# Making the two parts of w_out beside the projections, and sharing out the turned weights' parts anew

## The chip, the cores and the metric

One core of one Trainium2 chip runs the whole step as one program. The metric is the device time in microseconds (us) of one execution; what is compared are medians of several executions.

The engines are TensorE (PE, its weight loads PEld), VectorE (DVE), ScalarE (ACT), GpSimd (POOL) and SyncE (SP), which issues all DMAs of this kernel. Each engine works through its own instructions in one fixed order; an instruction whose input isn't there holds up all that stand behind it on that engine.

## The reference, cut to what matters

One layer of a hybrid backbone on 256 context tokens and 1024 latent tokens, width 1024. A combined projection of the normed input feeds a gated linear attention (GLA) and a differential attention; both are gated, concatenated and pass through one output projection:

```python
def diff_attention(q, k, v, lam):
    ...
        s = jnp.einsum('bqhid,bkhid->bihqk', qi, k).astype(jnp.float32) * scale
        p = jax.nn.softmax(s, axis=-1)
        a = p[:, 0] - lam * p[:, 1]
        return jnp.einsum('bhqk,bkhv->bqhv', a.astype(v.dtype), v)
...
    o = jnp.concatenate([og, od], axis=-1) * jax.nn.silu(gate)
    return jnp.einsum('blm,md->bld', o, w_out_l)
```

Everything is fp32. The kernel gets near fp32 precision from matmuls in a reduced fp32 format (F32R) by splitting each operand x into two parts, hi = F32R(x) and lo = F32R(x - hi), and adding three products: hi·hi, hi·lo and lo·hi.

## The kernel before, in words

**Stages.** A start (modulation, norm, the turned and split input `hhi`, `hlo`), then three mixes of projection work with GLA and other work (`MIX[0]` to `MIX[2]`, lines 1284 to 1300), then the attention of the latent tokens, into whose end the output projection reaches, and the rest of the output tiles.

**A mix.** `mix` takes one step of the generator named by each letter of a string: m is the projections (a unit of w_in is loaded, split and multiplied), a the GLA and the context tokens' attention, b a third one. In `MIX[1]` b is `cached()` (line 662): eight times it loads 256 KB of cached keys or values into `kqst` (tag s1), splits them with `split_store` (line 593: ACT copies to hi, the engine passed to it subtracts to lo, two DMAs store the parts to memory), in buffers of tags h1 and h2. These three tags have two buffers each, and the projections' own results pass through them. In the mixes a scheduler puts each engine's instructions in order, the strings giving the priority; `MIX[2]` has no b.

**The attention** (lines 1303 to 1508) is ordered by hand: with `manual_schedule` each engine keeps the order in which the instructions are written. Sixteen blocks (4 heads, 4 times 256 query tokens) are pipelined: iteration j goes through the tuple `ORDER`, and each step is done for block j plus its offset. A block has the scores (`score`, L1130), the maxima (`peak`, L1137, DVE), the exponentials (`expo`, L1142, ACT), the difference of the two maps (`combine`: L1149, L1150 and the long L1152, all DVE), and then six pairs of key tiles, 0 to 5. For each pair `turn` transposes on PE into one PSUM tile `tp` and `part` makes hi (`aTh`) and lo (`aTl`); `weigh` then multiplies them with the values. The tuple `PARTS` says who does it. With 'direct' ACT reads `tp` into hi and DVE subtracts from `tp`. Otherwise ACT first copies `tp` to `aT` (L1167, three buffers), the first letter says who makes hi from it (G: POOL, L1178; A: ACT, L1176) and the second who makes lo (L1181; G: POOL, V: DVE). `late` takes the second six entries for the last five blocks. The merge of a block has two POOL steps, `oc` (L1219, `merge4`) and `olo` (L1225, `merge5`).

In `ORDER` the steps that use POOL or feed it stand like this, with pair 2 turned at an iteration's very end and parted at the next one's very beginning:

```python
    ('part', -2, 2), ('weigh', -2, 0), ('slot', 0), ('turn', -2, 3), ('part', -2, 1), ...
    ('merge4', -3), ... ('part', -2, 4), ... ('merge5', -3), ... ('part', -2, 5), ... ('wo', 0, 8, 6, 14),
    ('turn', -1, 0), ... ('weigh', -2, 10), ('part', -1, 0), ('weigh', -2, 11), ...
    ('score', 0, 1, 1), ... ('merge1', -2), ('expo', 0, 1, 0), ('turn', -1, 2),
```

(`('part', -2, 3)` stands just before `('merge4', -3)`.) The two `wo` steps call `load_wo` in iterations 6 to 13: a DMA of 256 KB of w_out into a buffer of the ring of `aT`, then `woh` and `wol` on POOL (L1310, L1311), sixteen times in all. `FILL` says where matmuls of the output tiles are put between the steps, from iteration 16 on.

Of the kernel before, what the change touches and what calls it, by code (L numbers as in the profile page):

```python
# [101 lines left out]
def mix(pattern, main, *others):  # L102
# [4 lines left out]
    for g in gens.values():  # L107
# [14 lines left out]
    ('mmmmabmmmmammammbmammmmammmmabmbbmmmmmambambmmmmammmbmmmbmmbmamamammbmmbbmmabmmamammmmmbmm'),  # L122
    ('mmamamaaammaaabmmmmaaammaaambmmaammabmabaammaambamammbmmabammmmabammmamamaaaammabaabmaamma'),
    ('ammmmmmammammamaamammammmmaammammmammmamammammmmmammmmaammmmmmammmmammmamamamammmaammammmammmmmmamam'
     'aammmmmamammmammmammammmmmammmmaammmamammmaamammammmmmammammammmmaamammmmaaammmaaaammaaammmmamaamaaa'
     'mmamaaamaammaaamaaammamamamaaamaaamammmaaaamaamaaaaaamaammmmaaamammaammmamm'),
)

PARTS = ('direct', 'GG', 'AV', 'GG', 'GG', 'GG', 'direct', 'GG', 'AV', 'GG', 'GG', 'AG')

ORDER = (
    ('part', -2, 2), ('weigh', -2, 0), ('slot', 0), ('turn', -2, 3), ('part', -2, 1), ('slot', 0), ('merge2', -3),
# [45 lines left out]
def body(tc, nc, I, O, ctx):  # L178
# [33 lines left out]
    qs_d = [dram.tile([2, 2, P, NTOK], F32, name=f"qs_d{i}") for i in range(2)]  # L212
    vs_d = dram.tile([2, NKALL, 512], F32, name="vs_d")
    oh_d = dram.tile([2, 8, P, NTOK], F32, name="oh_d")


    def sigmoid_parts(dst, x, tmp):
# [17 lines left out]
    with psum:  # L235
# [429 lines left out]
        def cached():  # L665
# [6 lines left out]
            for t in range(4):  # L672
# [3 lines left out]
                split_store(r, [rows[0], rows[1]], 0, 512, 1.0, G)  # L676
                yield

        def modgate():

            ga = gp.tile([P, 2, 2, 512], F32, name="ga", tag="W", bufs=2)
            acc = [[ga[:, j, hf] for hf in range(2)] for j in range(2)]
            for kt in range(KT):
                wg = gp.tile([P, 2, 512], F32, name="wg", tag="att", bufs=2)
                for hf in range(2):
                    S.dma_start(wg[:, hf], I["w_mod"][kt * P:(kt + 1) * P, 2 * D + hf * 512:2 * D + (hf + 1) * 512])
                for j in range(2):
                    for hf in range(2):
                        src = wg[:, hf]
                        if kt == 0:  # L690
                            V.tensor_scalar(out=acc[j][hf], in0=src, scalar1=sic[:, kt, j:j + 1], scalar2=None,
                                            op0=ALU.mult)
                        else:
                            V.scalar_tensor_tensor(out=acc[j][hf], in0=src, scalar=sic[:, kt, j:j + 1],
                                                   in1=acc[j][hf], op0=ALU.mult, op1=ALU.add)
                yield
            for j in range(2):
                for hf in range(2):
                    cs = slice(hf * 512, (hf + 1) * 512)
                    ps = psL.tile([P, 2, 512], F32, name="gs", tag="lv")[0:1, 0]  # L700
                    T.matmul(ps, one, acc[j][hf], start=True, stop=True)
                    row = sp.tile([1, 512], F32, name="grow", tag="s2")
                    S.dma_start(row, I["bgate"][:, cs])
                    V.tensor_tensor(out=row, in0=ps, in1=row, op=ALU.add)
                    S.dma_start(ga_d[j:j + 1, cs], row)
                    yield
# [403 lines left out]
        class Block:  # L1110


            def __init__(self, job):
                self.h, self.c0, self.nk = job[:3]
                self.job = job
                self.npair = self.nk // 256
                self.late = 6 * (jobs.index(job) >= 11)

            def load(self):
                self.ks, self.vs = get_kv(self.job)  # L1120
# [34 lines left out]
            def turn(self, pr):  # L1155

                tp = psT.tile([P, 512], F32, name="tp")
                for i in range(2):
                    kt = pr * 2 + i
                    for qt in range(2):  # L1160
                        T.transpose(tp[:, i * N + qt * P:i * N + (qt + 1) * P], self.am[qt][:, kt * P:(kt + 1) * P], ident)  # L1161
                if PARTS[pr + self.late] == "direct":
                    full, hi = tp, ap_.tile([P, 512], F32R, name="aTh", bufs=5)
                    A.activation(hi, tp, AF.Copy)
                else:
                    full, hi = ap_.tile([P, 512], F32, name="aT", bufs=3), None
                    A.activation(full, tp, AF.Copy)  # L1167
                self.full[pr] = full, hi

            def part(self, pr):  # L1170

                full, hi = self.full.pop(pr)
                if hi is None:
                    hi = ap_.tile([P, 512], F32R, name="aTh", bufs=5)
                    if PARTS[pr + self.late][0] == "A":
                        A.activation(hi, full, AF.Copy)  # L1176
                    else:
                        G.tensor_scalar(out=hi, in0=full, scalar1=1.0, scalar2=0.0, op0=ALU.mult, op1=ALU.add)  # L1178
                lo = ap_.tile([P, 512], F32R, name="aTl", bufs=5)
                eng = G if PARTS[pr + self.late][1] == "G" else V  # L1180
                eng.tensor_tensor(out=lo, in0=full, in1=hi.bitcast(F32), op=ALU.subtract)  # L1181
                self.ab[pr] = hi, lo

# [78 lines left out]
        def first_block():  # L1262

            b = blocks[0]
            for qt in range(2):
# [21 lines left out]
                *[feat_unit(U_G + m, use_gate(m)) for m in range(4, 6)],  # L1287

                last_gates()),
            seq(backward, stagger([prompt(0), prompt(1)], PL), stagger([prompt(2), prompt(3)], PL), first_loads(), first_block(), prompt_gate()))  # L1290
        proj.close()
    psum.close()
    with ExitStack() as s3:
# [8 lines left out]
        def load_wo(m, hf):  # L1302
# [2 lines left out]
                wol[m] = wo.tile([P, D], F32R, name=f"wol{m}")  # L1305
            cs = slice(hf * 512, (hf + 1) * 512)
            hi, lo = woh[m][:, cs], wol[m][:, cs]
            r = ap_.tile([P, 512], F32, name="wo_r", tag="aT", bufs=3)
            S.dma_start(r, I["w_out"][SLOT[m] * P:(SLOT[m] + 1) * P, cs])
            G.tensor_scalar(out=hi, in0=r, scalar1=1.0, scalar2=0.0, op0=ALU.mult, op1=ALU.add)  # L1310
            G.tensor_tensor(out=lo, in0=r, in1=hi.bitcast(F32), op=ALU.subtract)  # L1311


        s3b = ExitStack()
# [221 lines left out]
```

## Time and profile before

| what | value |
|---|---|
| median of 3 runs | 982.35 us (981.92 to 984.94) |
| the profiled execution's own time | 980.46 us |
| its span, first to last instruction | 978.4 us |
| PE busy | 907.6 us, 93% of the span |
| DVE busy | 607.8 us, 62% |
| ACT busy | 461.1 us, 47% |
| POOL busy | 410.6 us, 42% |
| DMA | 157.91 MB, 160 GB/s over the span |

The shares are means over stages that have different limits: POOL is 42% busy in the whole, but 88% and more in slices 24 to 33 of the 40 into which the page cuts the span. The time is read stage by stage, and in the attention cycle by cycle.

### The profile page before, as it was taken

What the parts mean: (1) busy time and instruction counts of PE and PEld (TensorE: products, weight loads), DVE (VectorE), ACT (ScalarE), POOL (GpSimd) and SP (SyncE); (2) the same over time, 40 slices, a digit from 0 to 9 for tenths busy, and PEclk for the clock granted to TensorE, in tenths of its full rate; (3) what the DMA queues carried; (4) which work ended last, traced back from release to release, by engine and by line L of the source; (5) the groups of instructions that cost most, each with busy time, mean ns of one, the idle gap of its engine ahead of it and who ended that gap; (6) DMA issues with size and microseconds to landing.
All of it is one profiled execution on the core that took longest, in us unless ns stands there. A gap on an engine that the chain in (4) does not pass through costs nothing.

```text
span 978.4 us, 15886 instructions
## 1 busy us (share of the span) xinstructions
PE 907.6 (93%) x5894; PEld 766.4 (78%) x5894; DVE 607.8 (62%) x853; ACT 461.1 (47%) x882; POOL 410.6 (42%) x344
## 2 busy tenths in 40 slices
PE   6889999998999999899899999899988888999997
PEld 1489889976899897677787888788867677888886
DVE  3788952232267655876675646899888889722223
ACT  2454355344522323233334666687767677732122
POOL 0454223135302213342334000488999999752221
PEclk9899999999999999999999999999999999999999
DMA  8842754587744454453464563363345226137751
GB/s 292 324 151 73 225 172 131 151 266 240 253 151 124 149 160 140 132 165 115 135 202 150 191 213 99 113 185 104 118 163 142 84 80 210 43 108 235 232 167 65
DMA packets 146316, 157.91 MB, mean 161 GB/s; under 512 B 10168, under 2 KB 115768, under 8 KB 146240
## 3 DMA queue, kind: packets, MB, share of 16 engines
q1 hardware_dynamic: 146240, 156.91, 50.8%
q8 instruction: 46, 0.75, 0.3%
q14 instruction: 30, 0.25, 0.1%
HBM read 104.30 MB, written 52.57 MB: 160 GB/s over the span
## 4 chain that ended last, share of the span: by engine, by line
PE 51%; POOL 13%; DVE 11%; issue 10%; ACT 7%; DMA 6%; SPq 1%; POOLq 0%; ACTq 0%; DVEq 0%
PE acc L452 4%; PE acc L453 4%; PE acc L454 4%; PE sc L1347 4%; PE sc L1348 4%; PE sc L1349 4%; PE acc L528 3%; PE acc L530 3%; PE acc L529 3%; POOL aTh L1178 3%; PE lv L831 3%; ACT p L1142 3%; PE mp L324 3%; POOL wol L1311 2%; POOL woh L1310 2%
## 5 line engine op out<-in xcount | busy, mean ns | idle before, releaser
L452 PE MATMUL acc<-hhi,w_hi 128*128 128x512 f32 (+1 forms) x440 | 158.2, 359 | 0.0
L453 PE MATMUL acc<-hlo,w_hi 128*128 128x512 f32 (+1 forms) x440 | 156.2, 355 | 0.0
L454 PE MATMUL acc<-hhi,w_lo 128*128 128x512 f32 (+1 forms) x440 | 155.8, 354 | 0.0
L1137 DVE TENSOR_REDUCE sm<-sc 128x1 f32<-128x1536 f32 x60 | 105.0, 1752 | 12.1 <-PE sc L1130 12.1
L1130 PE MATMUL sc<-ks,q 128*128 128x512 f32 x360 | 98.0, 408 | 2.7 <-ACT p L1142 2.7
L1142 ACT ACTIVATE p<-sc,sm 128x1536 f32<-128x1536 f32 x60 | 92.4, 1539 | 9.1 <-DVE sm L1137 6.4
L528 PE MATMUL acc<-w_hi,hhi 128*128 128x256 f32 x320 | 93.6, 293 | 2.5 <-ACT kqst L477 2.4
L1181 POOL TENSOR_TENSOR aTl<-aT,aTh 128x512 fp32r<-128x512 f32 x64 | 93.7, 1464 | 4.9
L452 PEld LDWEIGHTS acc<-hhi,w_hi 128*128 128x128 f32 x440 | 83.6, 190 | 12.8 <-issue 1.9
L454 PEld LDWEIGHTS acc<-hhi,w_lo 128*128 128x128 f32 x440 | 83.4, 190 | 11.4 <-issue 0.2
L530 PE MATMUL acc<-w_hi,hlo 128*128 128x256 f32 x320 | 92.0, 288 | 0.0
L529 PE MATMUL acc<-w_lo,hhi 128*128 128x256 f32 x320 | 91.9, 287 | 0.0
L453 PEld LDWEIGHTS acc<-hlo,w_hi 128*128 128x128 f32 x440 | 83.7, 190 | 10.4 <-issue 0.2
L1178 POOL TENSOR_SCALAR aTh<-aT 128x512 fp32r<-128x512 f32 x59 | 61.2, 1037 | 39.5 <-ACT aT L1167 38.0
L1130 PEld LDWEIGHTS sc<-ks,q 128*128 128x128 f32 x360 | 64.2, 191 | 13.7 <-ACT p L1142 3.0
L528 PEld LDWEIGHTS acc<-w_hi,hhi 128*128 128x128 f32 x320 | 62.7, 196 | 8.1 <-ACT kqst L477 2.6
L1167 ACT ACTIVATE aT<-tp 128x512 f32<-128x512 f32 x80 | 47.8, 598 | 39.9 <-PE tp L1161 19.0
L1161 PE MATMUL tp<-ident,p 128*128 128x128 f32 x360 | 54.7, 274 | 11.8 <-ACT aT L1167 11.8
L1347 PE MATMUL sc<-woh,oh 128*128 128x512 f32 (+1 forms) x168 | 65.0, 387 | 0.0
L1349 PE MATMUL sc<-woh,oh 128*128 128x512 f32 (+1 forms) x168 | 64.6, 384 | 0.0
L1348 PE MATMUL sc<-wol,oh 128*128 128x512 f32 (+1 forms) x168 | 64.6, 384 | 0.0
L1192 PE MATMUL ov<-aTl,vs 128*128 128x256 f32 x192 | 56.3, 293 | 8.3 <-POOL aTl L1181 7.7
(309 smaller groups left out, 2128.1 us busy)
## 6 DMA issues: line engine op xcount, KB each, us to landing
w_raw<-w_u SPq DMA_DIRECT2D x29, 512.0 KB, 3.6
oh<-oh_d SPq DMA_DIRECT2D x20, 512.0 KB, 4.2
wm<-w_mod SPq DMA_DIRECT2D x16, 512.0 KB, 5.0
q<-qs_d SPq DMA_DIRECT2D x64, 128.0 KB, 2.9
ks<-ks_d SPq DMA_DIRECT2D x4, 1536.0 KB
vs<-vs_d SPq DMA_DIRECT2D x8, 768.0 KB, 5.6
xt<-x_all SPq DMA_DIRECT2D x10, 512.0 KB, 10.2
x<-x_all SPq DMA_DIRECT2D x10, 512.0 KB, 4.7
```

The source lines that it names most:

```text
L452: T.matmul(ps, w_h, hhi[bi][:, kt, ts], start=kt == 0, stop=False)
L453: T.matmul(ps, w_h, hlo[bi][:, kt, ts], start=False, stop=False)
L454: T.matmul(ps, w_l, hhi[bi][:, kt, ts], start=False, stop=kt == KT - 1)
L528: T.matmul(ps, h_h, w_h, start=kt == 0, stop=False)
L529: T.matmul(ps, h_h, w_l, start=False, stop=False)
L530: T.matmul(ps, h_l, w_h, start=False, stop=kt == KT - 1)
L1130: T.matmul(sc[:, k0:k0 + w], self.q[:, a, sub, qt * P:(qt + 1) * P], self.ks[:, sub, k0:k0 + w], start=a == 0, stop=a == 1)
L1137: V.tensor_reduce(out=self.sm[qt][:, sub:sub + 1], in_=self.sc[qt, sub], op=ALU.max, axis=AX.X, negate=True)
L1142: A.activation(p_, self.sc.pop((qt, sub)), AF.Exp, bias=sm[:, sub:sub + 1], accum_out=self.s0[:, qt:qt + 1] if sub == 0 else sm[:, 2:3])
L1347: T.matmul(ps, oh[:, 0, m], woh[m][:, cs], start=m == 0, stop=False)
L1348: T.matmul(ps, oh[:, 0, m], wol[m][:, cs], start=False, stop=False)
L1349: T.matmul(ps, oh[:, 1, m], woh[m][:, cs], start=False, stop=m == 7)
```

## The change

A generator `wo_parts` is added as b of `MIX[2]`, where sixteen b's are set into the unchanged row of m's and a's. It loads each half row block of w_out, splits it with `split_store` (hi on ACT, lo on POOL) and stores both parts to memory (`wo_d`). `load_wo` brings the two parts back with two DMAs of 256 KB and does no arithmetic. `PARTS` has one set of six entries for all blocks: pair 2 goes from 'AV' to 'GG', and pair 5 from 'GG' to 'AG' (which the last five blocks had already).

```diff
-PARTS = ('direct', 'GG', 'AV', 'GG', 'GG', 'GG', 'direct', 'GG', 'AV', 'GG', 'GG', 'AG')
+PARTS = ('direct', 'GG', 'GG', 'GG', 'GG', 'AG')
...
+    wo_d = dram.tile([2, 8, P, D], F32, name="wo_d")
...
+        def wo_parts():
+
+            for m in range(8):
+                for hf in range(2):
+                    r = sp.tile([P, 512], F32, name="kqst", tag="s1")
+                    cs = slice(hf * 512, (hf + 1) * 512)
+                    S.dma_start(r, I["w_out"][SLOT[m] * P:(SLOT[m] + 1) * P, cs])
+                    split_store(r, [wo_d[0, m], wo_d[1, m]], hf * 512, 512, 1.0, G)
+                    yield
...
-                self.late = 6 * (jobs.index(job) >= 11)
...
-                if PARTS[pr + self.late] == "direct":
+                if PARTS[pr] == "direct":
...
-                    if PARTS[pr + self.late][0] == "A":
+                    if PARTS[pr][0] == "A":
...
-                eng = G if PARTS[pr + self.late][1] == "G" else V
+                eng = G if PARTS[pr][1] == "G" else V
...
-            r = ap_.tile([P, 512], F32, name="wo_r", tag="aT", bufs=3)
-            S.dma_start(r, I["w_out"][SLOT[m] * P:(SLOT[m] + 1) * P, cs])
-            G.tensor_scalar(out=hi, in0=r, scalar1=1.0, scalar2=0.0, op0=ALU.mult, op1=ALU.add)
-            G.tensor_tensor(out=lo, in0=r, in1=hi.bitcast(F32), op=ALU.subtract)
+            S.dma_start(hi.bitcast(F32), wo_d[0, m, :, cs])
+            S.dma_start(lo.bitcast(F32), wo_d[1, m, :, cs])
```

In `MIX[2]` the first b stands after 70 m's and 31 a's, the last after 151 of 164 m's and 100 of 111 a's. `ORDER` and `FILL` are as before.

## Rows read from the trace of the kernel before

**Rows 1.** The page, part 2: busy tenths of POOL in 40 slices
```profile
POOL 0454223135302213342334000488999999752221
```

**Rows 2.** Windows cut at starts of the aTh behind oc; busy us by engine
```profile
core 0: us, PE busy (x) PEld busy (x) DVE busy (x) ACT busy (x) POOL busy (x), PEclk, DMA share, GB/s
629.67:643.64 13.97, 13.55 (x92) 12.21 (x91) 13.62 (x16) 11.76 (x20) 11.56 (x9) 1.00 0.93 264
643.64:687.69 44.05, 41.45 (x272) 36.80 (x271) 39.51 (x43) 35.68 (x61) 35.51 (x30) 1.00 0.42 129
687.69:822.91 135.22, 117.14 (x728) 98.86 (x727) 116.51 (x113) 97.10 (x162) 128.41 (x112) 1.00 0.41 124
822.91:836.91 14.00, 13.16 (x86) 11.61 (x85) 13.09 (x15) 11.70 (x22) 11.30 (x10) 1.00 0.54 168
836.91:866.52 29.61, 29.61 (x194) 26.59 (x193) 16.57 (x20) 19.48 (x36) 22.28 (x19) 1.00 0.09 28
```

**Rows 3.** Timeline of POOL: its first step in the attention, and one cycle
```profile
start us, us, engine line op out<-in xcount [idle before <-releaser]
622.83 0.62 POOL L1178 TENSOR_SCALAR aTh<-aT 128x512 fp32r<-128x512 f32 x1 [26.32 <-ACT aT L1167]
...
675.11 1.29 POOL L1181 TENSOR_TENSOR aTl<-aT,aTh 128x512 fp32r<-128x512 f32 x1
676.37 0.74 POOL L1225 TENSOR_TENSOR olo<-oc,ohi 128x256 fp32r<-128x256 f32 x1
677.07 0.62 POOL L1178 TENSOR_SCALAR aTh<-aT 128x512 fp32r<-128x512 f32 x1
677.78 1.27 POOL L1181 TENSOR_TENSOR aTl<-aT,aTh 128x512 fp32r<-128x512 f32 x1
679.10 0.62 POOL L1178 TENSOR_SCALAR aTh<-aT 128x512 fp32r<-128x512 f32 x1
679.80 2.69 POOL L1181 TENSOR_TENSOR aTl<-aT,aTh 128x512 fp32r<-128x512 f32 x1
683.90 0.62 POOL L1178 TENSOR_SCALAR aTh<-aT 128x512 fp32r<-128x512 f32 x1 [1.41 <-ACT aT L1167]
684.60 1.28 POOL L1181 TENSOR_TENSOR aTl<-aT,aTh 128x512 fp32r<-128x512 f32 x1
686.90 0.74 POOL L1219 TENSOR_TENSOR oc<-oc,gt 128x256 f32<-128x256 f32 x1 [1.01 <-DVE sm L1149]
```

**Rows 4.** Timeline of ACT, the same stretches
```profile
624.67 0.60 ACT L1167 ACTIVATE aT<-tp 128x512 f32<-128x512 f32 x1
...
679.90 0.38 ACT L1200 ACTIVATE oc<-ov 128x256 f32<-128x256 f32 x1 [0.88 <-PE ov L1192]
680.18 1.54 ACT L1142 ACTIVATE p<-sc,sm 128x1536 f32<-128x1536 f32 x1
...
681.81 0.60 ACT L1167 ACTIVATE aT<-tp 128x512 f32<-128x512 f32 x1
```

**Rows 5.** Timeline of DVE, the same cycle
```profile
679.54 1.82 DVE L1152 SCALAR_TENSOR_TENSOR p<-p,sm,p 128x1536 f32<-128x1536 f32 x1
...
683.17 0.69 DVE L1181 TENSOR_TENSOR aTl<-aT,aTh 128x512 fp32r<-128x512 f32 x1
...
686.39 0.43 DVE L1218 TENSOR_TENSOR oc<-oc,sq 128x256 f32<-128x256 f32 x1
```

**Rows 6.** Timeline of PE, the same cycle
```profile
679.10 0.39 PE L1192 MATMUL ov<-aTl,vs 128*128 128x256 f32 x1 [0.48 <-POOL aTl L1181]
...
687.71 0.29 PE L1192 MATMUL ov<-aTl,vs 128*128 128x256 f32 x1
```

**Rows 7.** Groups of instructions by line: busy us, mean ns, idle us before them
```profile
L1311 POOL TENSOR_TENSOR wol<-wo_r,woh 128x512 fp32r<-128x512 f32 x16 | 23.6, 1476 | 1.3
L1310 POOL TENSOR_SCALAR woh<-wo_r 128x512 fp32r<-128x512 f32 x16 | 19.3, 1204 | 0.0
...
L600 POOL TENSOR_TENSOR klo<-kqst,khi 128x512 fp32r<-128x512 f32 x8 | 11.3, 1415 | 19.3 <-ACT khi L598 19.3
...
L598 ACT ACTIVATE khi<-kqst 128x512 fp32r<-128x512 f32 x8 | 5.0, 629 | 7.3 <-DMA kqst<-cv 4.4 <-DMA kqst<-ck 2.9
```

**Rows 8.** Windows, columns as in Rows 2: the cached parts' stretch, and the changed mix
```profile
200.00:262.00 62.00, 57.30 (x331) 44.82 (x330) 19.46 (x39) 30.67 (x56) 23.10 (x19) 1.00 0.79 260
430.00:590.00 160.00, 152.70 (x990) 129.00 (x989) 102.97 (x158) 70.82 (x148) 38.07 (x28) 0.99 0.52 165
```

More of the change, by code (lines that the diff above doesn't have):

```diff
@@ L124 @@
     ('ammmmmmammammamaamammammmmaammammmammmamammammmmmammmmaammmmmmammmmammmamamamammmaammammmammmmmmamam'
-     'aammmmmamammmammmammammmmmammmmaammmamammmaamammammmmmammammammmmaamammmmaaammmaaaammaaammmmamaamaaa'
-     'mmamaaamaammaaamaaammamamamaaamaaamammmaaaamaamaaaaaamaammmmaaamammaammmamm'),
+     'abammmmmamambmmammmammabmmmmmammmmbaammmamammbmaamammammbmmmammammabmmmmaamammbmmaaammmaabaammaaammm'
+     'bmamaamaaambmamaaamaambmaaamaaammbamamamaaambaaamammmaabaamaamaaaabaamaammmmaaamammaammmamm'),
 )
-PARTS = ('direct', 'GG', 'AV', 'GG', 'GG', 'GG', 'direct', 'GG', 'AV', 'GG', 'GG', 'AG')
+PARTS = ('direct', 'GG', 'GG', 'GG', 'GG', 'AG')
 ORDER = (
@@ L1289, in body @@
                 last_gates()),
-            seq(backward, stagger([prompt(0), prompt(1)], PL), stagger([prompt(2), prompt(3)], PL), first_loads(), first_block(), prompt_gate()))
+            seq(backward, stagger([prompt(0), prompt(1)], PL), stagger([prompt(2), prompt(3)], PL), first_loads(), first_block(), prompt_gate()), wo_parts())
         proj.close()
```

## The prediction, made before the changed kernel ran

> **What bounds the kernel now.** I read the page's row of busy tenths first: POOL stands at 8 and 9 only in slices 24 to 33, the attention; elsewhere it has room [rows 1]. There I cut windows at the start of the first aTh behind oc, once in each iteration, so that a window's length is a cycle's length [rows 2]. The first cycle (iteration 2 to 3) lasts 13.97 us, the next three 44.05 / 3 = 14.68, the eight that make parts of w_out 135.22 / 8 = 16.90, the one behind them 14.00; the last two (29.61 us) hold matmuls of the output tiles, and PE is busy all through. That is 207.2 us for 13 cycles. In the eight POOL is busy 128.41 of 135.22 us and PE 117.14: POOL is the bound. In the others PE is nearest to it (41.45 of 44.05) with DVE close (39.51), and POOL has 2.8 us of idle time a cycle. What the loads of w_out cost today is thus 8 × (16.90 - 14.68) = 17.8 us, and that is the most that taking them away could give by itself.
>
> In one such cycle I then read who waits for whom. In order of time POOL does [rows 3]: lo of pair 4 (675.11), olo, pair 5 (677.07 and 677.78), then at once pair 1 (679.10, 679.80), a wait of 1.41 us for ACT, pair 3 (683.90, 684.60), oc. Pair 2 isn't there: it is ACT's and DVE's (DVE 683.17, [rows 5]). Two things matter. First, lo of pair 1 took 2.69 us and not 1.28. DVE's L1152 had started at 679.54 while hi of pair 1 ran (to 679.72), ended at 681.36, and POOL's waiting lo was through at 682.49: the two don't run together, and the one that waits goes ahead of the other's next step. It costs POOL 2.69 - 1.28 = 1.41 us. Second, pair 2's copy aT, the last step of an iteration's turns, ran 681.81 to 682.41 [rows 4], 3.36 us behind the end of pair 5's lo (677.78 + 1.27 = 679.05). That is no accident: PE waits for that lo (679.10, 0.48 us idle [rows 6]), does the rest of pair 5, ACT then copies the block's sum (oc, 679.90), does an exponential (680.18), and only then comes that aT.
>
> **The attention, part by part.** Removed: woh and wol, 16 × (1.20 + 1.48) = 42.9 us of POOL [rows 7]. Added: hi and lo of pair 2 on POOL, 16 × (0.62 + 1.28) = 30.4 us; removed for pair 5: 11 × 0.62 = 6.8 us. By sums of busy time POOL loses 19 us, and DVE 16 × 0.69 = 11 us. But `ORDER` is unchanged, and in it pair 2's part is the first step of an iteration, ahead of pair 1's. Today this costs POOL nothing. Now POOL does hi of pair 2 first, and that needs the aT that comes 3.36 us behind lo of pair 5. Pair 1, which today fills this gap, is queued behind it, and pairs 3 and 4, oc, olo and pair 5's lo behind that. So each cycle holds a closed loop: aT of pair 2, all eleven POOL steps, lo of pair 5, PE, ACT, the next aT of pair 2. Its length from the rows:
>
> - from aT's end to POOL's start 0.09 us (as at 683.90, with pair 3's aT);
> - 4 hi at 0.70 from start to start (677.07 to 677.78), 5 lo at 1.26 (675.11 to 676.37), olo 0.70, oc 0.75: 2.80 + 6.30 + 1.45 = 10.55 us [rows 3];
> - one L1152 in this stretch, 1.41 us. It can't fall into the gap, as it waits for L1218, which stands 3.98 us behind aT's end (686.39 - 682.41), when POOL is at work. The other L1152 of the iteration falls into the gap (today 679.54, 0.49 behind lo of pair 5). L1218 itself (0.43 us) holds POOL some 0.3 us [rows 5];
> - back from lo of pair 5 to aT: 3.36 us.
>
> Sum 15.7 us. It hangs on one tie. Pair 3's hi is due at 0.09 + 2 × (0.70 + 1.26) = 4.01, L1218 at 3.98. If L1218 comes first, L1152 gets in ahead of pair 3's lo, which is then done some 7.7 us behind aT; PE wants it 5.3 us behind (687.71 - 682.41 [rows 6]) and, with its other waits, about 6.3 to 6.9. That stall of about 0.8 us is passed on to the cycle: 16.5. I take 15.9, between the two and nearer to the sum. Bounds: 14.00, the shortest that a cycle has been with pair 5's hi on ACT, and 16.90, a cycle with both parts of w_out. So 13 cycles take 13 × 15.9 = 206.7 us against 207.2: the eight long cycles give back what the five short ones lose. -0.5 us, with ends 13 × 14.0 - 207.2 = -25 and 13 × 16.9 - 207.2 = +12.5.
>
> At the attention's start POOL's first hi waits for pair 2's aT, 624.67 + 0.60 + 0.09 = 625.36, and not for pair 1's at 622.83 [rows 3, 4]: +2.5 us (0 to 3). In the last two cycles PE is full today [rows 2]; the loop, with fewer exponentials in it, is about as long as they are, and I take +1.5 (0 to 3). The attention in all: +3.5 us.
>
> The Trainium skill weighs on this (SBUF — State Buffer, Who interferes with whom): a DVE instruction with two SBUF inputs and a GpSimd one that reads SBUF exclude each other for the whole instruction. The 2.69 us agrees. The lo of pair 2 on DVE was such an instruction, so by the rule moving it to POOL spares POOL up to 0.69 us a cycle, 9 us over 13. By the row it spares nothing in a short cycle: at 683.17 POOL was waiting for ACT until 683.90.
>
> **The loads back.** 32 DMAs of 256 KB in place of 16, in iterations 6 to 13, straight into their own tiles: 8 MB in 135 us, where the DMA engines are 41% busy [rows 2]. The output tiles need them long after, so 0. That a load no longer takes a buffer of the ring of aT is part of the 17.8 us.
>
> **The projections.** Sixteen times: a load of 256 KB, hi on ACT (0.63 us), lo on POOL (1.42 with its waits), two stores [rows 7]. In the changed stretch ACT is busy 70.8 of 160 us and POOL 38.1; 10 and 23 us more have room. PE is busy 152.7 of 160, so work beside it is hidden unless it holds up PE's chain [rows 8]. Three ways remain: ACT waits for the load with all behind it (for the cached parts 7.3 us in 8 steps), POOL's lo excludes DVE, which is busy 103 of 160 and carries the GLA chain, and SP's queue, in which a store waits for its hi ahead of the loads behind. The nearest measure is the same work in the mix before: in its 62 us PE sat idle 4.7 us, with eight such steps in it. All of it put down to them gives 0.59 each, 9.4 for sixteen; the other end is 0. Part of that idle time is the GLA pass's own, so I take 3.
>
> **Sum.** -0.5 + 2.5 + 1.5 + 3 = +6.5 us on the profiled execution's own 980.46, 987. That execution lay 1.9 us under the median; on the median, 982.35 + 6.5 = 989.
>
> **Rivals.**
> (a) The loop doesn't close: L1152 runs while POOL is idle, or the aT comes earlier, so that the loop falls to 14.7 or less (it needs only 1.0 us off) and PE is the bound again at 14.68. For it: POOL's own steps are but 10.55 us, and DVE has 0.69 less. Against it: the order on POOL, and that L1152 is behind L1218. Then 13 × 14.68 - 207.2 = -16.4, and +3 for the projections: -13.4, 969. This is the other side, faster; it decides below a cycle of about 15.2.
> (b) The tie always falls well and the work beside the projections is free: cycles of 15.6, 13 × 15.6 - 207.2 = -4.4, +4 at the ends, 0 to 1: 982 to 983, no change.
> (c) The sixteen steps beside the projections are paid in full, as in the mix before: +3.5 + 9.4 = +13, 995; with a tie that always falls badly 1002. For it: SP and ACT in order; against it: the wide slack of ACT and POOL there.
>
> **How the numbers follow.** Forecast (985 to 993) 0.45, (a) 0.22, (b) 0.18, (c) 0.15. About 0.3%, 2.9 us, is what a measurement can tell from no change. Faster: (a) and a little of the forecast's low side, 0.25; same: (b), 0.18; slower 0.57. The range goes from 971, into (a), to 999, into (c).
>
> **What would show it.** In the changed trace POOL's hi of pair 2 should wait some 3 us for ACT's aT in each cycle, just behind lo of pair 5, and the order pair 2, 1, 3 follow without a gap; cycles should be equal, 15.6 to 16.5 us, with and without the loads of w_out. PE should wait for lo of pair 5 longer than 0.48 us. Cycles near 14.7 in all iterations would prove (a). In the mix, PE's idle time over 430 to 590 should grow from 7.3 us by about 3; growth near 9 is (c).

## The result and the profile after

The changed kernel takes 1011.35 us (median of 4 executions, 1009.45 to 1013.47) against 983.17 (981.92 to 984.94): ratio 1.0286, 95% interval 1.0257 to 1.0315. It is slower by 28 us; the forecast was 989, the range ended at 999. The profiled execution took 1013.47 us, 33.0 more than that of before.

Windows of the changed kernel, cut as in [rows 2] at starts of the aTh behind oc, and behind them the changed mix's stretch of [rows 8]:

```profile
core 0: us, PE busy (x) PEld busy (x) DVE busy (x) ACT busy (x) POOL busy (x), PEclk, DMA share, GB/s
648.61:673.11 24.50, 19.69 (x127) 16.91 (x127) 18.62 (x19) 16.12 (x25) 18.25 (x16) 1.00 0.82 225
...
722.71:868.95 146.24, 125.83 (x807) 109.92 (x805) 119.35 (x117) 106.48 (x180) 107.13 (x101) 1.00 0.34 100
868.95:899.93 30.98, 30.53 (x195) 26.86 (x194) 15.44 (x17) 16.90 (x32) 23.16 (x24) 1.00 0.09 27
430.00:590.00 160.00, 148.15 (x961) 123.52 (x960) 102.07 (x152) 71.70 (x147) 53.41 (x40) 0.99 0.65 206
```

Twelve cycles, 673.11 to 868.95, take 195.84 us, 16.32 each; in [rows 2] the same twelve took 836.91 - 643.64 = 193.27. So +2.6. From the first aTh to the aTh behind the first oc it is 24.50 against 643.64 - 622.83 = 20.81 [rows 2, 3], +3.7; the last two cycles 30.98 against 29.61, +1.4. The attention lost 7.7 us. The larger loss stands ahead of it: its first aTh starts at 648.61 and not at 622.83 [rows 3], +25.8.

No engine is the bound of a cycle now: POOL is busy 107.13 of 146.24 us, PE 125.83. The page shows it too (busy tenths of POOL; [rows 1] had eights and nines):

```profile
POOL 0454223224203123324343112358686776762221
```

The timeline of POOL shows why, the end of a cycle in which a tie (below) falls badly and a cycle in which it falls well:

```profile
701.89 0.89 POOL L1188 TENSOR_SCALAR aTh<-aT 128x512 fp32r<-128x512 f32 x1
702.86 2.80 POOL L1191 TENSOR_TENSOR aTl<-aT,aTh 128x512 fp32r<-128x512 f32 x1
...
708.97 1.30 POOL L1191 TENSOR_TENSOR aTl<-aT,aTh 128x512 fp32r<-128x512 f32 x1
714.58 0.62 POOL L1188 TENSOR_SCALAR aTh<-aT 128x512 fp32r<-128x512 f32 x1 [4.31 <-ACT aT L1177]
...
719.19 1.33 POOL L1191 TENSOR_TENSOR aTl<-aT,aTh 128x512 fp32r<-128x512 f32 x1
```

The row at 708.97 is lo of pair 5; the next instruction, hi of pair 2, waits 4.31 us for ACT's copy aT. ACT's timeline has that copy third behind the block's sum, as in [rows 4]:

```profile
712.01 0.39 ACT L1210 ACTIVATE oc<-ov 128x256 f32<-128x256 f32 x1
712.29 1.54 ACT L1152 ACTIVATE p<-sc,sm 128x1536 f32<-128x1536 f32 x1
...
713.90 0.60 ACT L1177 ACTIVATE aT<-tp 128x512 f32<-128x512 f32 x1
```

DVE's timeline shows the tie, between pair 3's lo on POOL and DVE's L1228 with L1162 behind it (in the kernel before these are L1218 and L1152):

```profile
701.88 0.43 DVE L1228 TENSOR_TENSOR oc<-oc,sq 128x256 f32<-128x256 f32 x1
...
702.72 1.82 DVE L1162 SCALAR_TENSOR_TENSOR p<-p,sm,p 128x1536 f32<-128x1536 f32 x1
...
718.71 0.67 DVE L1228 TENSOR_TENSOR oc<-oc,sq 128x256 f32<-128x256 f32 x1 [0.32 <-ACT sq L1225]
...
719.79 2.34 DVE L1162 SCALAR_TENSOR_TENSOR p<-p,sm,p 128x1536 f32<-128x1536 f32 x1
```

At 702.72 L1162 started before pair 3's lo (702.86), which then took 2.80 us; at 719.79 the lo was already running (719.19) and took 1.33. POOL pays all the same, at oc (2.25 us at 720.48), but by then PE has its lo. Of the 13 cycles that end at the oc of 672.42 to 868.25, ten have a lo of 2.8 us in this place and three don't. From one aTh behind oc to the next the twelve cycles are 15.67 to 16.62 us long; from one hi of pair 2 to the next it is 16.60 us behind a tie that fell badly (681.37 to 697.97) and 15.47 behind one that fell well (714.58 to 730.05). PE pays for it (its timeline):

```profile
701.98 0.39 PE L1202 MATMUL ov<-aTl,vs 128*128 128x256 f32 x1 [0.85 <-POOL aTl L1191]
...
705.72 0.39 PE L1202 MATMUL ov<-aTl,vs 128*128 128x256 f32 x1 [1.26 <-POOL aTl L1191]
```

The first is lo of pair 1 (done at 701.92), for which PE waits 0.85 us in each cycle; the second is lo of pair 3, in the ten cycles alone. For lo of pair 5, which ended at 710.27, PE does not wait: its next idle time is 0.39 us ahead of 714.55, for a copy aT.

In the page's groups over the whole kernel (busy us, mean ns, idle before them), POOL waits 81.8 us for the copies aT (21.0 of it ahead of its first hi in the attention, at 648.61) and PE 25.8 us for lo:

```profile
L1202 PE MATMUL ov<-aTl,vs 128*128 128x256 f32 x192 | 57.3, 298 | 26.2 <-POOL aTl L1191 25.8
L1188 POOL TENSOR_SCALAR aTh<-aT 128x512 fp32r<-128x512 f32 x64 | 44.0, 688 | 81.8 <-ACT aT L1177 81.8
```

Ahead of the attention the gates of the projections come late. ACT's timeline at the mix's end (`khi` here is the split of w_out; `la` is a gate's first step, whose buffer is of the same tag s1 as `kqst`):

```profile
614.33 0.60 ACT L653 ACTIVATE la<-acc 128x512 f32<-128x512 f32 x1 [1.27 <-POOL klo L601]
...
621.85 0.42 ACT L1072 ACTIVATE poh<-poc 128x256 fp32r<-128x256 f32 x1 [3.46 <-DVE poc L1069]
622.17 0.62 ACT L599 ACTIVATE khi<-kqst 128x512 fp32r<-128x512 f32 x1
624.42 0.60 ACT L653 ACTIVATE la<-acc 128x512 f32<-128x512 f32 x1 [1.64 <-POOL klo L601]
...
627.64 0.60 ACT L653 ACTIVATE la<-acc 128x512 f32<-128x512 f32 x1 [0.82 <-POOL klo L601]
```

Three times `la` waits until POOL has read the buffer that a step of w_out holds. At 622.17 that step's `khi` had itself been queued behind a 3.46 us wait of another chain. The gate holds PE's accumulator until DVE's `gt`, and PE's timeline has this behind it:

```profile
630.25 0.58 PE L453 MATMUL acc<-hhi,w_hi 128*128 128x256 f32 x1 [5.07 <-DVE gt L660]
```

How much is lost there can be read where PE's work is the same. From the 125th last matmul into `acc`, the projections' accumulator, to the last one PE does some 150 matmuls, scores of the prompts among them. Windows of that, of the kernel before, the changed one, and of two of the experiments below (f5_ring, i1_nos1), columns as above:

```profile
583.75:612.57 28.82, 28.71 (x150) 23.98 (x148) 18.53 (x23) 18.11 (x32) 2.18 (x3) 1.00 0.35 108
592.82:635.09 42.27, 33.00 (x150) 27.11 (x149) 20.58 (x27) 22.27 (x41) 7.96 (x8) 0.88 0.58 194
584.98:620.98 36.00, 31.65 (x150) 26.01 (x149) 20.25 (x26) 21.87 (x39) 2.21 (x3) 0.91 0.65 211
589.95:618.72 28.77, 28.77 (x151) 23.97 (x150) 17.73 (x23) 18.30 (x32) 4.91 (x5) 1.00 0.65 208
```

The changed kernel loses 13.5 us in it: 9.2 are idle time of PE, and 4.3 are the lower granted clock, at which the same work keeps PE busy 33.00 us and not 28.71.

### The profile page after: what moved, and what is told of

Same layout as the page of the kernel before. It is cut to its first block, busy times and chain, and to the rows that moved or that the text cites. A ratio compares the mean times of both kernels' runs of the same rounds, so it can differ in the third digit from the quotient of the medians.

```text
span 1011.7 us, 16024 instructions
## 1 busy us (share of the span) xinstructions
PE 913.3 (90%) x5894; PEld 770.5 (76%) x5894; DVE 598.5 (59%) x837; ACT 466.0 (46%) x893; POOL 399.1 (39%) x349
## 4 chain that ended last, share of the span: by engine, by line
PE 42%; POOL 16%; DMA 12%; issue 10%; DVE 10%; ACT 8%; SPq 2%; POOLq 0%; DVEq 0%; ACTq 0%
POOL aTl L1191 8%; PE sc L1140 3%; PE acc L529 3%; PE acc L531 3%; PE acc L530 3%; PE lv L842 3%; PE acc L453 3%; PE acc L454 3%; PE acc L455 3%; PE tp L1171 2%; PE sc L1355 2%; POOL aTh L1188 2%; PE sc L1357 2%; PE sc L1356 2%; ACT p L1152 2%
## 5 line engine op out<-in xcount | busy, mean ns | idle before, releaser
L1191 POOL TENSOR_TENSOR aTl<-aT,aTh 128x512 fp32r<-128x512 f32 x80 | 119.6, 1495 | 5.7 <-ACT aTh L1186 0.4
L1152 ACT ACTIVATE p<-sc,sm 128x1536 f32<-128x1536 f32 x60 | 92.4, 1540 | 8.9 <-DVE sm L1147 8.9
L1202 PE MATMUL ov<-aTl,vs 128*128 128x256 f32 x192 | 57.3, 298 | 26.2 <-POOL aTl L1191 25.8
L1188 POOL TENSOR_SCALAR aTh<-aT 128x512 fp32r<-128x512 f32 x64 | 44.0, 688 | 81.8 <-ACT aT L1177 81.8
L601 POOL TENSOR_TENSOR klo<-kqst,khi 128x512 fp32r<-128x512 f32 x24 | 31.5, 1312 | 87.7 <-ACT khi L599 76.6
```

The source lines that it names most:

```text
L1152: A.activation(p_, self.sc.pop((qt, sub)), AF.Exp, bias=sm[:, sub:sub + 1], accum_out=self.s0[:, qt:qt + 1] if sub == 0 else sm[:, 2:3])
```

## The experiments

Three numbers stand for each: the ratio of the medians to before; the stretch from the attention's first aTh on POOL to its last oc (before 266.74 us); and the loss ahead of it, which is the difference of the medians less that of the stretch (what lies behind the last oc is 90.6 to 91.5 us in all). I take the loss from the medians because the profiled execution of before reached the attention early: the two kernels that leave the mixes as they were, e1_parts_only and g3_partsorder, have their first aTh 4.5 and 4.9 us later than it, and by the medians lose 1.1 and -0.7. So this reckoning is good to some 1 to 2 us.

| kernel | time, us | ratio, 95% interval | stretch | ahead |
|---|---|---|---|---|
| after | 1011.35 | 1.0286 (1.0257 to 1.0315) | 273.7 | +21.2 |
| e1_parts_only | 1001.12 | 1.0170 (1.0131 to 1.0208) | 283.0 | +1.1 |
| e2_wo_only | 980.33 | 0.9962 (0.9939 to 0.9985) | 249.5 | +13.9 |
| e3_order | 977.97 | 0.9931 (0.9909 to 0.9952) | 246.0 | +14.9 |
| g3_partsorder | 988.80 | 1.0054 (1.0033 to 1.0075) | 273.0 | -0.7 |
| e5_copy | 992.53 | 1.0074 (1.0049 to 1.0100) | 271.3 | +4.2 |
| f1_early | 972.18 | 0.9902 (0.9866 to 0.9937) | 246.0 | +10.4 |
| f2_poolhi | 977.41 | 0.9950 (0.9922 to 0.9978) | 246.0 | +15.6 |
| f3_mix1 | 1001.10 | 1.0185 (1.0142 to 1.0227) | 246.0 | +39.3 |
| f5_ring | 969.81 | 0.9872 (0.9822 to 0.9922) | 246.1 | +7.9 |
| g1_inplace | 977.49 | 0.9934 (0.9908 to 0.9960) | 246.0 | +15.1 |
| g2_hring | 967.69 | 0.9837 (0.9797 to 0.9877) | 246.1 | +5.2 |
| g4_earlypool | 975.60 | 0.9937 (0.9910 to 0.9964) | 246.7 | +12.4 |
| h1_act | 970.15 | 0.9877 (0.9850 to 0.9904) | 246.3 | +8.3 |
| h2_pool | 971.38 | 0.9893 (0.9869 to 0.9918) | 246.1 | +9.6 |
| h3_dvelo | 977.08 | 0.9950 (0.9929 to 0.9971) | 246.2 | +15.2 |
| h4_earlydve | 972.70 | 0.9913 (0.9879 to 0.9947) | 246.3 | +10.8 |
| i1_nos1 | 969.95 | 0.9872 (0.9844 to 0.9900) | 246.1 | +7.3 |
| i2_earlynos1 | 981.09 | 0.9984 (0.9964 to 1.0004) | 246.1 | +18.4 |

### The attention: which part of the change, and is it the order?

**e1_parts_only**: before, with the new `PARTS` alone.

```diff
-PARTS = ('direct', 'GG', 'AV', 'GG', 'GG', 'GG', 'direct', 'GG', 'AV', 'GG', 'GG', 'AG')
+PARTS = ('direct', 'GG', 'GG', 'GG', 'GG', 'AG') * 2
```

> Edit: the kernel before with the new PARTS alone (w_out still split on POOL in iterations 6 to 13). Theory M (the loss is made by the sixteen steps beside the projections and at the handover to the attention, the attention's loop adds only some 8 us): cycles without loads of w_out about 16.3 us as in the changed kernel, cycles with them 16.5 to 18.5 as the loads' 3.8 us on POOL fall into the 3.4 us in which POOL waits for pair 2's aT; the first aTh as early as before (622.8); 992 to 1005 us. Rival P (the new PARTS is what costs most of the 28 us, and the mix only moves it): 1006 us or more.

**e2_wo_only**: the changed kernel with the old `PARTS` and `late`; w_out's parts still made beside the projections.

```diff
-PARTS = ('direct', 'GG', 'GG', 'GG', 'GG', 'AG')
+PARTS = ('direct', 'GG', 'AV', 'GG', 'GG', 'GG', 'direct', 'GG', 'AV', 'GG', 'GG', 'AG')
...
+                self.late = 6 * (jobs.index(job) >= 11)
...
```

> Edit: the changed kernel with the old PARTS (both halves of the tuple, with late). Theory M: the attention runs at its old cycles without loads of w_out, 14.7 and 14.0 us, from the first aTh to oc of iteration 17 about 222 to 226 us (before 242.9, changed 250.6), and the loss ahead of it stays, first aTh at 640 to 649: 984 to 992 us, no better than before although POOL is relieved. Rival P: the loss ahead of the attention shrinks as well, 965 to 975.

**e3_order**: the changed kernel with pair 1's part ahead of pair 2's.

```diff
-    ('part', -2, 2), ('weigh', -2, 0), ('slot', 0), ('turn', -2, 3), ('part', -2, 1), ('slot', 0), ...
+    ('weigh', -2, 0), ('slot', 0), ('part', -2, 1), ('part', -2, 2), ('turn', -2, 3), ('slot', 0), ...
```

> Edit: the changed kernel with ORDER changed at its head, the parts of pair 1 ahead of those of pair 2 and both ahead of the turn of pair 3. Loop theory (POOL stands still behind pair 5's lo until pair 2's aT comes, with pair 1 queued behind): pair 1 fills that gap again and cycles fall from 16.3 to 14.0 to 15.0 us, 13 of them give back 17 to 30 us: 982 to 995 us. Rival (POOL's sum of work or the lock with DVE is the bound, whatever the order): cycles stay above 15.8, 1004 us or more.

The new `PARTS` alone lengthen the attention's stretch by 16.3 us, moving w_out alone shortens it by 17.3, and both together give +7.0. So the two don't add up: with w_out moved, the new `PARTS` cost 24.2 us (249.5 to 273.7). Swapping two steps in `ORDER` brings the changed kernel's stretch to 246.0. Windows of e3_order, columns as above:

```profile
678.37:692.87 14.50, 14.11 (x98) 12.74 (x96) 13.00 (x14) 12.32 (x21) 13.03 (x12) 1.00 0.83 256
692.87:835.57 142.70, 137.93 (x900) 122.38 (x899) 127.47 (x131) 117.69 (x201) 130.93 (x112) 1.00 0.41 121
```

and its POOL, from lo of pair 5 on:

```profile
711.20 1.29 POOL L1191 TENSOR_TENSOR aTl<-aT,aTh 128x512 fp32r<-128x512 f32 x1
713.07 0.62 POOL L1188 TENSOR_SCALAR aTh<-aT 128x512 fp32r<-128x512 f32 x1 [0.58 <-ACT aT L1177]
713.77 2.66 POOL L1191 TENSOR_TENSOR aTl<-aT,aTh 128x512 fp32r<-128x512 f32 x1
716.40 0.62 POOL L1188 TENSOR_SCALAR aTh<-aT 128x512 fp32r<-128x512 f32 x1
```

Ten cycles of 14.27 us with PE busy 137.93 of 142.70: PE is the bound. The wait of 4.3 us is one of 0.58, as pair 1 fills the gap and L1162 falls on pair 1's lo (2.66). That the order is the cause is shown: it was undone and the cycle fell by 2 us. With the order put right the new `PARTS` are worth 3.5 us of the stretch (e2_wo_only 249.5, e3_order 246.0). Both kernels came out below the times expected of them (984 and more, 982 and more).

**g3_partsorder**: e1_parts_only with the order of e3_order; w_out stays in the attention.

> Before, with the new PARTS for all blocks and the changed order of e3_order, and w_out split on POOL in the attention as before. Tells whether the moving of w_out is needed once the order is right. If POOL is the bound of the cycles with loads (17.4 us of steps, as e1_parts_only showed), they stay at 17.0 to 17.5 and the five others fall to 14.3: 5 x 14.3 + 8 x 17.3 = 210 us for 13 cycles against 207.2, time 984 to 988, no faster than before. If the wait for pair 2's copy was all, every cycle falls to 14.3 to 15.5 and the time is 960 to 970.

988.8, just above what was expected from POOL's busy time. The stretch is 273.0 us, so the right order does not pay without moving w_out: in its cycles with loads POOL has no gap left (window of it, columns as above):

```profile
692.35:835.50 143.15, 120.62 (x734) 103.98 (x733) 105.90 (x105) 97.16 (x163) 137.74 (x121) 0.96 0.40 117
```

### Ahead of the attention: transfers, place, engines

**e5_copy**: the changed kernel, but each step is two copies from memory to memory, with no buffer and no arithmetic.

```diff
-                    S.dma_start(r, I["w_out"][SLOT[m] * P:(SLOT[m] + 1) * P, cs])
-                    split_store(r, [wo_d[0, m], wo_d[1, m]], hf * 512, 512, 1.0, G)
+                    for a_ in range(2):
+                        S.dma_start(wo_d[a_, m][:, cs], I["w_out"][SLOT[m] * P:(SLOT[m] + 1) * P, cs])
```

> Edit: the changed kernel, but the sixteen steps copy w_out twice from memory to memory (32 DMAs of 256 KB in place of 48) and make no parts, so hi and lo are both w_out itself; no buffer of s1, h1, h2, no ACT and no POOL. Theory B (the loss ahead of the attention comes through the shared buffers and ACT's and POOL's orders): first aTh back at 623 to 628, and with the attention's loop left, 988 to 996 us. Rival D (the DMAs and SP's queue make it): first aTh stays at 638 or later, 1002 us or more.

The loss ahead falls from 21.2 to 4.2, with the reloads and the order of the attention as in the changed kernel. Of the 4.2, 2.9 are the wait of POOL's first hi for pair 2's copy (pair 1's is done at 629.67, pair 2's at 632.60). So what cost were the steps in the third mix, not the reloads. It does not say whether it was their transfers or what they do on the core, because the copies, which wait for no buffer, were not made in that mix: SP issues all of them in the first one (its view of `wo_d`, first and last start):

```profile
L686 SPq DMA_DIRECT2D wo_d<-w_out x32: 490/596/2225, 61.4 to 131.0; - x32
```

All that follow have the order of e3_order.

**f5_ring**: the load into `kqst` and two stores from it, no ACT, no POOL, no h1 and h2.

```diff
-                    split_store(r, [wo_d[0, m], wo_d[1, m]], hf * 512, 512, 1.0, G)
+                    for a_ in range(2):
+                        S.dma_start(wo_d[a_, m][:, cs], r)
```

> Edit: e3_order, but each step loads w_out into its buffer of s1 and stores that twice, with no parts made (hi and lo are both w_out itself): s1, the 48 DMAs and SP's queue stay, h1, h2, ACT and POOL are out of it. Theory R1 (s1 is what the gates wait for): first aTh at 636 to 644, 973 to 980. Theory A or h1 and h2: near the bare copies, 625 to 630, 961 to 967.

+7.9: half of e3_order's 14.9 stays with bare transfers through s1 (the parts are not made). The mix's end takes 36.00 us in place of 28.82 (above), so nearly all of it lies there: a gate's `la` waits 10.4 us, once, until a store has read the buffer.

**f1_early**: the full steps of e3_order, their sixteen b's one behind every fourth m from the start of `MIX[2]` on.

```diff
-    ('ammmmmmammammamaamammammmmaammammmammmamammammmmmammmmaammmmmmammmmammmamamamammmaammammmmammmmmamam'
+    ('ammmmbmmmammbammamaambammammbmmaammbammmambmmamambmammmbmmmammbmmaammbmmmmbammmmbammmambamamammmbmaam'
...
```

> Edit: e3_order with the sixteen steps early in MIX[2], one behind every fourth m from the 4th to the 64th (the cut ended at the 151st). Place theory (the steps cost what they do because they stand in the last 60 us ahead of the attention, where gates, first scores and loads follow each other): first aTh at 623 to 632 and 958 to 968 us, faster than the kernel before by 1.5 to 2.5%. Rival (each step costs its 1.2 us wherever it stands in this mix): first aTh stays at 638 to 646, 974 to 982.

**f3_mix1**: the full steps in `MIX[1]`, as sixteen more b's behind those of `cached()`; `MIX[2]` has none.

```diff
-            seq(pass_a(), few(backward, 1)), cached())
+            seq(pass_a(), few(backward, 1)), seq(cached(), wo_parts()))
```

> Edit: e3_order with the sixteen steps in MIX[1], behind the eight of the cached parts, and MIX[2] as in the kernel before. Place theory: the handover is as before, the cost is what the mix before has left, 0.6 us a step, up to 9.4 us: first aTh at 623 to 634, 958 to 970. Rival (1.2 us a step anywhere): 638 to 646, 974 to 982.

The row of b's in `MIX[1]` was set anew for all the steps, so that the cached parts' eight loads, too, start earlier (200.3 to 233.8 us, before 203.1 to 255.9).

The same sixteen steps cost much or little by their place. Early in the third mix it is +10.4, between the two ranges expected, and with an interval that overlaps e3_order's; in the mix before it is +39.3, where I had counted room: in two of its windows PE is busy 49.70 of 62 us (57.30 before, [rows 8]) at a granted clock of 0.86, and 70.07 of 88.

```profile
200.00:262.00 62.00, 49.70 (x260) 38.56 (x258) 12.95 (x26) 22.66 (x43) 23.95 (x21) 0.86 0.78 261
262.00:350.00 88.00, 70.07 (x512) 61.78 (x510) 41.32 (x63) 32.38 (x60) 21.99 (x17) 0.84 0.66 217
```

PE waits 14.6 us of these for `gt` at the accumulator, in six waits; the kernel before has none there.

**f2_poolhi**: e3_order with hi of w_out on POOL too, ACT has no part.

```diff
-                    split_store(r, [wo_d[0, m], wo_d[1, m]], hf * 512, 512, 1.0, G)
+                    hi = sp.tile([P, 512], F32R, name="khi", tag="h1")
+                    lo = sp.tile([P, 512], F32R, name="klo", tag="h2")
+                    G.tensor_scalar(out=hi, in0=r, scalar1=1.0, scalar2=0.0, op0=ALU.mult, op1=ALU.add)
+                    G.tensor_tensor(out=lo, in0=r, in1=hi.bitcast(F32), op=ALU.subtract)
...
```

> Edit: e3_order with hi of the parts of w_out on POOL, so that ACT has no part in the sixteen steps; places and buffers as they were. Theory A (ACT waits for the loads of w_out with the gates' steps behind it): first aTh at 626 to 634, 962 to 970 us. Theory R (the shared buffers s1, h1 and h2 are held up by the steps): first aTh stays at 638 to 646, 974 to 982.

**g4_earlypool**: the edits of f1_early and f2_poolhi together.

> The changed order, the sixteen steps early in the third mix (as f1_early, one after every 4th projection step), and their hi on POOL (as f2_poolhi). If the two gains add (12.7 and 17.1 ahead of the attention against 19.4 late with ACT), the first aTh comes at 632 to 634 and the time is 968 to 971. If early it is the DMAs that cost, ACT's part is nothing and the time stays at 971 to 974.

ACT's wait for the load was not the cost: with hi on POOL the loss is 15.6 late and 12.4 early, no less than with hi on ACT, and g4_earlypool lies above both of its ranges.

### Work or buffers

Between f5_ring (+7.9) and e3_order (+14.9) lie the buffers h1 and h2 and the work on two engines. The next four take them apart.

**g1_inplace**: f5_ring, and ACT and POOL work on the tile in place (the parts are not made).

```diff
+                    A.activation(r.bitcast(F32R), r, AF.Copy)
+                    G.tensor_tensor(out=r.bitcast(F32R), in0=r, in1=r, op=ALU.add)
                     for a_ in range(2):
                         S.dma_start(wo_d[a_, m][:, cs], r)
```

> The order changed as in e3_order, and each of the sixteen steps loads its half block into kqst (tag s1), ACT copies it onto itself, POOL adds it to itself in place, and the tile is stored twice: the work of ACT and POOL, and no buffer of tags h1 and h2. (Both stored parts are twice w_out; the parts proper are left out.) With the bare ring and no ACT or POOL work (f5_ring) the first aTh of the attention came at 631.6 and the time was 969.8; with parts in h1 and h2 (e3_order) at 642.2 and 978.0. Theory R: those 10 us come of the two buffers each of h1 and h2, through which the projections' own results pass: first aTh at 631 to 635, time 969 to 972. Theory W: they come of the work itself on ACT and POOL, each in one fixed order: 640 to 644, 976 to 980. Between (636 to 639): both.

**g2_hring**: loads straight into buffers of h1 and h2 and stores from there (no s1, and the parts are not made).

```diff
+                    for a_ in range(2):
+                        r = sp.tile([P, 512], F32, name=f"wor{a_}", tag=f"h{a_ + 1}")
+                        S.dma_start(r, I["w_out"][SLOT[m] * P:(SLOT[m] + 1) * P, cs])
+                        S.dma_start(wo_d[a_, m][:, cs], r)
...
```

> The other half of the same cross: each step takes a buffer of h1 and one of h2, loads w_out straight into both and stores both; no ACT, no POOL, no kqst (64 DMAs in place of 48; both stored parts are w_out, the splitting is left out). Theory R (the projections wait for buffers of h1 and h2): first aTh at 638 to 645, time 975 to 981. Theory W (the work on ACT and POOL): 629 to 634, time 968 to 972.

**h1_act** and **h2_pool**: g1_inplace with one of the two instructions only (h1_act without the second line of that diff, h2_pool without the first).

> g1_inplace without POOL's instruction: each step loads into kqst, ACT copies the tile onto itself, it is stored twice (the splitting is left out). The transfers alone cost some 5 to 8 us by the medians (g2_hring 967.7, f5_ring 969.8), with ACT's and POOL's work in place 977.5. Theory A, the cost of the work is ACT's, which waits for the load with all that stands behind it: ratio to before 0.992 to 0.996, as g1_inplace. Theory G, it is POOL's, whose reads hold up DVE: 0.982 to 0.988, as f5_ring. In the middle (0.989 to 0.991): both.

> The other half: each step loads into kqst, POOL adds the tile to itself in place, it is stored twice; ACT has no part (the splitting is left out). Theory A: ratio 0.982 to 0.988. Theory G: 0.992 to 0.996. That f2_poolhi, with both parts on POOL, was no better than e3_order speaks for G.

At this place h1 and h2 are innocent (g2_hring +5.2), against my theory R. But the work isn't a sum either: ACT's instruction alone adds 0.4 to f5_ring's 7.9, POOL's 1.7, both 7.2. The intervals of these ratios are some 2.5 us wide to either side (f5_ring's 5), so that the two singles are not told apart, while the pair's median is outside theirs. h1_act came out as theory G had it, h2_pool between the two.

**h3_dvelo** and **h4_earlydve**: e3_order and f1_early with `V` in place of `G`, so that lo is DVE's.

```diff
-                    split_store(r, [wo_d[0, m], wo_d[1, m]], hf * 512, 512, 1.0, G)
+                    split_store(r, [wo_d[0, m], wo_d[1, m]], hf * 512, 512, 1.0, V)
```

> e3_order with lo of w_out's parts on DVE in place of POOL (hi on ACT; the full parts). Theory G: without POOL's reads the steps cost what the transfers cost and 16 x 0.7 = 11 us of DVE, which has 60 of 160 us free in the mix: 0.985 to 0.990, 968 to 973. Theory A: as e3_order, 0.992 to 0.996.

> f1_early (steps early in the third mix) with lo of w_out's parts on DVE (the full parts). Theory G: 966 to 970. Theory A: 971 to 974, as f1_early.

Both fell on the side of theory A, against which h1_act speaks: without POOL the loss stays at 15.2 and 10.8. So neither engine is it. What the costly kernels at the late place have in common (e3_order, f2_poolhi, g1_inplace, h3_dvelo: 14.9 to 15.6) is two instructions, one behind the other, between the load into s1 and the buffer's release.

**i1_nos1**: the same full work, load, place and stores, with the chain in buffers of h1 and h2 alone.

```diff
-                    r = sp.tile([P, 512], F32, name="kqst", tag="s1")
+                    r = sp.tile([P, 512], F32, name="klo", tag="h2")
...
+                    hi = sp.tile([P, 512], F32R, name="khi", tag="h1")
+                    A.activation(hi, r, AF.Copy)
+                    G.tensor_tensor(out=r.bitcast(F32R), in0=r, in1=hi.bitcast(F32), op=ALU.subtract)
```

> e3_order, with the full parts made without kqst (tag s1): w_out is loaded into the buffer of h2, ACT copies it to hi in h1, POOL subtracts in place in h2, both are stored. Work, transfers and place are those of e3_order. So far every kernel whose step has two engine instructions one behind the other between load and store stands at 0.993 to 0.995 of before, whichever engines they are on (e3_order, f2_poolhi, g1_inplace, h3_dvelo), and every one with one or none at 0.984 to 0.989. Theory S: it is the time for which a step holds one of the two buffers of s1, through which the gates' and the rotated features' results go; the two instructions make it longer. Then without s1: 0.984 to 0.989, 967 to 972. Theory C: it is the chain itself, wherever its buffers are: 0.992 to 0.996, 975 to 979.

969.95, a loss of 7.3 in place of 14.9, as theory S said. The idle time of ACT and DVE ahead of the instructions on `la` in the stretch 430 to 640, by what ended it (us, times), shows it. Before:

```profile
  ACT la L654: 12.9, 9
  PE acc L454: 9.1, 7
```

After (e3_order has the same 3.7 us for `klo`):

```profile
  ACT la L655: 17.2, 9
  PE acc L455: 5.7, 3
  POOL klo L601: 3.7, 3
```

g1_inplace, where the buffer is held until both stores are through (its profiled execution is 3.8 us below its median):

```profile
  DMA wo_d<-kqst: 15.2, 5
  ACT la L655: 10.9, 8
  PE acc L455: 2.1, 1
```

i1_nos1:

```profile
  ACT la L655: 13.3, 8
  PE acc L455: 6.8, 5
```

In i1_nos1 no gate waits for a step of w_out, as in the kernel before, and PE's stall for `gt` at the accumulator is gone.

The mix's end says the same, more sharply than the medians. In the profiled executions the stretch of the 125 last matmuls into `acc` (above) takes 28.8 to 29.0 us in each kernel that holds no buffer of s1 for w_out there: before, e1_parts_only, g3_partsorder, e5_copy, g2_hring, i1_nos1, and all with the steps elsewhere. It takes 35.2 to 36.0 with s1 and no or one instruction (f5_ring, h1_act, h2_pool) and in g1_inplace, and 38.4 to 42.3 with the full steps through s1 (f2_poolhi, h3_dvelo, e2_wo_only, e3_order, after). i1_nos1 loses nothing in it with the same work, and with the DMA engines as busy as in f5_ring (0.65 both), so neither the work nor the traffic is the cause there, but the hold on s1. One thing is left in this: the scheduler orders PE's scores and projections there somewhat differently from kernel to kernel, and what part of the loss comes through that order was not taken apart.

**i2_earlynos1**: the edit of i1_nos1 on f1_early.

> The same early in the third mix (f1_early without s1, full parts). Theory S: 0.982 to 0.988, 965 to 971, better than both kernels and than f1_early. Theory C: as f1_early, 0.989 to 0.993.

A miss: +18.4, worse than f1_early's +10.4. Early in the mix it is the value projections that use h1 and h2, and here h2 is held from the load on. Waits of i2_earlynos1 in 262 to 430:

```profile
ACT khi L686 <- DMA klo<-w_out: 35.2, 9, 8.2
...
ACT vhi L587 <- DMA wo_d<-khi: 4.8, 3, 1.9
...
DVE vlo L588 <- DMA wo_d<-klo: 4.5, 3, 1.7
```

and of f1_early:

```profile
ACT khi L597 <- DMA kqst<-w_out: 19.4, 4, 5.7
```

The values' own splits (`vhi`, `vlo`) wait for w_out's stores, and ACT waits 35.2 us for the loads of w_out. That fits theory S, with the other pair of buffers, but it was read after the run, and no run tried a chain with buffers of its own at this place.

**What is open.** Three kernels without the chain in s1 still lose 5 to 8 us ahead of the attention. Of f5_ring's 7.9, 7.2 lie at the mix's end, where it holds s1. g2_hring (5.2, with an interval of 4 to either side) and i1_nos1 (7.3) lose nothing there, and where theirs lie isn't shown; SP's queue and the load on the DMA engines weren't tried. After's own loss (21.2) is 6 us above e3_order's, of which the start of the attention explains 2.6 (below). The rest isn't in the third mix: from the 800th last matmul into `acc`, ahead of the first step of w_out, to the last, the two profiled executions take 248.3 and 247.9 us.

## Why the prediction was wrong

- **The loop closes, but by another path.** POOL's hi of pair 2 waits for ACT's aT in each cycle (predicted some 3 us, measured 4.3, and 3.4 where the tie had fallen well), cycles are equal with and without reloads of w_out, and the order is the cause (e3_order). Rival (a), 14.7 a cycle, and (b) fall. One sign did not come: PE was to wait longer than 0.48 us for lo of pair 5, and it doesn't wait for it. The late hi of pair 2 reaches PE sooner, through lo of pair 1 (0.85 us of idle time in each cycle) and of pair 3 (1.26 in the ten bad ones); from there PE's own work leads to the next aT. The sum over all eleven steps of POOL and back from lo of pair 5 was thus not the path that bounds the cycle, and that its 15.7 lies near the 15.47 measured is in part luck.
- **The tie** was predicted as 15.7 or 16.5 and taken at 15.9; the runs show 15.47 and 16.60. It fell badly in 10 of 13, and the mean of twelve cycles is 16.32. That makes +2.6 for these where I had -0.5 for 13. The Trainium skill's rule (SBUF — State Buffer, Who interferes with whom) that the two kinds of instruction exclude each other agrees: 2.80 us for a lo beside L1162, 1.33 for one that was under way before it.
- **The ends.** The last two cycles cost +1.4 (predicted 1.5). At the start the first aTh now waits for pair 2's copy (predicted 2.5; here pair 1's copy was done at 645.93 and pair 2's at 648.53, so 2.6), and from there to the aTh behind the first oc it takes 3.7 us more, which I had not counted.
- **The step that failed is the term of the projections**: +3, with 9.4 as its upper end, for which the runs show 13.9 (e2_wo_only), 14.9 (e3_order) and, in the changed kernel itself, up to 18.6 (21.2 less 2.6). The measured 28.2 us are these 18.6, the 2.6 and the 7.0 of the stretch, against 3, 2.5 and 1.0 in the forecast: most of what it lacks is here. Rival (c), that they are paid in full, had the right sign and the wrong price. Two things were wrong in it. I took my upper end from PE's idle time in another mix [rows 8], with eight steps among other users of the rings; f3_mix1 shows that sixteen steps cost 39 there and f1_early 10 early in the third. And I looked at 430 to 590: there PE's idle time did grow from 7.3 to 11.85, by 4.6, near the 3 that I had named. The rest, 13.5 us, came at the mix's end, behind 590, where the last of the steps stand between the gates and the prompts' chains; 4.3 of it is the clock that fell with PE's idle time. I had weighed ACT's and POOL's free time, in which nothing was short. What was short were the two buffers of s1: half of the loss (14.9 to 7.3), and all of it at the mix's end (41.61 us to 28.77), goes when the steps don't hold one.
- **The removed loads** were worth what I had put on them: 17.8 us, and e2_wo_only's stretch is 17.3 shorter. In the changed kernel the new `PARTS` took more than that back (24.2, from e2_wo_only to after), through a step of `ORDER` that nobody had touched.

The version to keep is i1_nos1, at 969.95 us, 0.9872 of before (0.9844 to 0.9900); f1_early, 972.18, and h4_earlydve, 972.70, are as good within the intervals. All have the order of e3_order.

## What to carry to other kernels

When work moves between in-order engines, write down who is first in each queue and close the loop: a step that costs nothing on one engine can hold up all that stands behind it on another. Work put beside other work is priced by what it holds, for how long and in whose way, at the place where it ends up (a ring of two buffers, a queue), and not by the free time of its engines. Look for its cost over the whole stretch and to its end: here 13.5 of 18.6 us lay behind the window that I had meant to watch.

## What I had not expected of the hardware

This stall of PE cost more than its length. Windows of the changed kernel around its 5.07 us of idle time:

```profile
625.00:630.00 5.00, 0.19 (x2) 0.00 (x0) 1.24 (x2) 4.12 (x9) 1.27 (x1) 0.80 0.47 173
630.00:635.00 5.00, 4.75 (x23) 4.75 (x24) 2.37 (x5) 2.13 (x6) 0.00 (x0) 0.52 0.42 147
635.00:640.00 5.00, 3.81 (x20) 2.70 (x18) 2.70 (x4) 1.77 (x5) 0.00 (x0) 1.00 0.59 173
```

In the window behind it the granted clock is 0.52, nearly all of it at the lower level of 1.2 GHz; then it is back at full. Had those 4.75 us been granted in full they would have held about 4.75 × 0.52 = 2.5 us of work, so by this estimate the stall cost some 2.3 us more. The matmuls' own pace gives about the same: in that window those of 128x256 start 0.21 us apart, ahead of the stall 0.12, which makes some 2 us.
